# One exponential per head for the decay matrices, attention values two query blocks at a time, and modulated weights for the last down products

## The chip, the cores and the metric

The kernel runs on one core of a Trainium2 chip. The metric is the device time of one execution in microseconds. The engines are named as the profile names them: PE is TensorE (PEld its weight loads), DVE is VectorE, ACT is ScalarE, POOL is GpSimd, and SP issues the DMAs.

## The reference

One transformer block on 1024 tokens of width 1024. The parts that matter here:

```python
def _dilated_branch(q, k, v, rel_bias, window, dilation):
    ...
    s = jnp.einsum('bhrnqd,bhrnkd->bhrnqk', qb * dh ** -0.5, kw) + bias[None, :, None, None]
    s = jnp.where(valid, s, NEG_INF)
    ...
    o = jnp.einsum('bhrnqk,bhrnkd->bhrnqd', e, vw) / denom

def _chunk_gated_delta_rule(q, k, v, g, beta):
    ...
    diff = gcum[..., :, None] - gcum[..., None, :]
    decay = jnp.where(causal, jnp.exp(jnp.where(causal, diff, 0.0)), 0.0)
    k_beta = kc * bc[..., None]
    a_mat = jnp.where(strict, jnp.einsum('nbhcd,nbhed->nbhce', k_beta, kc) * decay, 0.0)
    ...
    qk = jnp.where(causal, jnp.einsum('nbhcd,nbhed->nbhce', qc, kc) * decay, 0.0)

def reference(...):
    ...
        y = jnp.concatenate([y_attn, y_delta], axis=-1) @ w_out[l]
        x = x + g1 * y
        h = _rmsnorm(x, norm_ffn_g[l]) * (1.0 + sc2) + sh2
        y = (jax.nn.silu(h @ w_gate[l]) * (h @ w_up[l])) @ w_down[l]
        x = x + g2 * y
    return _rmsnorm(x, final_norm_g)
```

`k` is l2-normalised per head before the delta rule, and the rows of `a_mat` and `qk` carry that norm's reciprocal root.

## The kernel before

The kernel is written against a tile framework that orders instructions ahead of time. Every instruction has a priority, its place in the program; a block under `urgent()` goes 6000 places ahead. A scheduler steps through a model of the chip and emits, on each engine, the ready instruction of the highest priority. The order so found is fixed: on the chip each engine runs its instructions in that order and waits wherever an operand is late. `tc.issue_after(ins)` ties an instruction behind another one on the same engine.

The work comes in stages. The first 100 us form the first projections. Then come two groups `g` of the gated delta rule, four heads each (`delta(0)`, `delta(1)`), then attention over four pairs of heads (`attend`), the output projection, the second norm, and the feed-forward network as seven products of a fast 2x2 scheme (`up_...` and `down`). The remaining projections of the input are a pool of filler, the generators behind `fill`. `ahead(us)` and `turn(name)` pull an amount of it into PE's stream where the table `FILL` has an entry, and attention draws what is left.

**Decay matrices.** For each group `delta_rows` (L697 on) broadcasts the cumulated gate G of each head over the partitions by a DMA into a tile `dt` of 128x8x128, and `affine_select` on POOL (L712) puts -1e30 below the diagonal. `delta_prep` (L750 on) takes the logarithm of the squared norms of k (`Ln`, L761, for group 0 at L1235), halves and negates it (L762), gets `rk` from it by `Exp` (L763) and subtracts G of the partition's own token (L764). The result `lr` is a bias per partition, one column per chunk and head, so 32 activations of 128x128 follow per group (L767): exp(G of the column + lr). Behind them on ACT stand two activations `eb` (L835). From `rk` come `nbp` (L771), which PE transposes (L777), `nbg` and `kds`. PE then forms the kk products (L796) and DVE multiplies them with the decay matrices (L802). POOL scales q with `eb` in place (L836). Conv and `Silu` of v stand in `delta_v` (L553, L557).

**Attention values.** A unit is a pair of heads `hp` and a block `qb` of 128 queries. `attend` runs score (L1325), softmax, transposes (L1349) with their copies into `et` tiles (L1352, L1354), and value products (L1366), the last three units behind the score. A unit's value products are 2(qb+1) matmuls of 128x64 by 128x128, the two heads e alternating and writing PSUM partitions 64e to 64e+63. Four `et` buffers exist, two to a unit.

**The last down products.** `down(i, ...)` runs one of seven products over 11 slices f; `down_parts` loads a slice of activations and weights and splits each into a high and a low part (L1603, L1604), and `down_mm` (L1809) makes three matmuls for each of four banks. In the last call, `down(6, ..., final=True)`, the last TAIL = 4 slices run bank by bank, each bank followed by its end: multiply with the gate g2 (L1858), add the residual (L1859), square with a sum (L1861), add the two half sums (L1867), root (L1868), reciprocal (L1869), scale (L1874, L1876) and store.

Of the kernel before, what the change touches and what calls it, by code (L numbers as in the profile page):

```python
# [18 lines left out]
P = 128  # L19
T = 1024  # L20
D = 1024
# [13 lines left out]
AHEADF = 3  # L35
XB, ETB, AT, AV = 5, 4, 1, 3
EPS = 1e-6
# [45 lines left out]
def build(tc, I, out):  # L83
# [466 lines left out]
    def conv(ci, xp, dst):  # L550
        nc.scalar.activation(dst, xp, AF.Copy, scale=cw[:, ci, 3:4])
        for s_ in range(1, 4):
            nc.vector.scalar_tensor_tensor(  # L553
                out=dst[:, s_:T], in0=xp[:, 0 : T - s_], scalar=cw[:, ci, 3 - s_ : 4 - s_], in1=dst[:, s_:T],
                op0=ALU.mult, op1=ALU.add,
            )
        nc.scalar.activation(dst, dst, AF.Silu)  # L557

# [138 lines left out]

    sel = {}

    def delta_rows(g):  # L700

        dts = []
        for hl_ in range(4):
# [10 lines left out]
                base=0, channel_multiplier=-1,  # L714
            )
            dts.append(dt_)
        return dts

    def delta_norms(g):
        n = {}  # L720
        for name in ("rk", "eq", "nbp", "nbg", "kds", "lr"):
            n[name] = pd.tile([P, 8, 4], F32, name=f"{name}{g}", tag=name, bufs=2)
        return n
# [26 lines left out]
    def delta_prep(g, st, norms, kt, lts):  # L750

        rk, eq, nbp, nbg, kds, lr = (norms[k] for k in ("rk", "eq", "nbp", "nbg", "kds", "lr"))
        gs = slice(32 * g, 32 * g + 32)
# [5 lines left out]

        if g == 1:  # L760
            nc.scalar.activation(lr, rk, AF.Ln, bias=eps1)  # L761
        nc.vector.tensor_scalar(out=lr, in0=lr, scalar1=-0.5, scalar2=None, op0=ALU.mult)  # L762
        nc.scalar.activation(rk, lr, AF.Exp)  # L763
        nc.vector.tensor_tensor(out=lr, in0=lr, in1=g3(Gc), op=ALU.subtract)  # L764
        for h in range(4):
            for n in range(8):
                nc.scalar.activation(lts[h][:, n], lts[h][:, n], AF.Exp, bias=lr[:, n, h : h + 1])  # L767
        nc.vector.tensor_scalar(
# [442 lines left out]
    def delta_early():  # L1211

        for j in range(4):
            kind, q = ("k", j) if j < 2 else ("q", j - 2)
            t = pr.tile([P, T], F32, name=f"cv{j}", tag="dt", bufs=2)
            conv((4 if kind == "k" else 0) + 2 + q, fetch(j, f"{kind}{2 + q}"), t)
            delta_turn(1, kind, q, t, norms=norms[1])
            nc.sync.dma_start(_.cv[j], t)
# [4 lines left out]
    def delta(g):  # L1223
        st = {}
        kt = []
        for j in range(4):
# [4 lines left out]
            if g == 0:  # L1231
                conv((4 if kind == "k" else 0) + hp, xps[j], t)
                kt.append(delta_turn(g, kind, q, t, norms=norms[0], keep=kind == "k"))
                if j == 1:
                    nc.scalar.activation(norms[0]["lr"], norms[0]["rk"], AF.Ln, bias=eps1)  # L1235
            else:
# [119 lines left out]

    def att_value(hp, qb, ets):
        va = loaded[hp][0]
        if qb % 4 == 0:
            ybanks[hp] = ybank(f"y{hp}_{qb}")  # L1360
        yps = ybanks[hp]
        yc = slice((qb % 4) * P, (qb % 4 + 1) * P)
        with turn(f"y{hp}_{qb}"):
            for kb in range(qb + 1):
                for e in range(2):
                    nc.tensor.matmul(  # L1366
                        yps[64 * e : 64 * e + 64, yc], va[:, kb, 64 * e : 64 * e + 64], ets[e][:, kb, :],
                        start=(kb == 0), stop=(kb == qb),
                    )
        if qb % 4 == 3:  # L1370
            cs = slice((qb - 3) * P, (qb + 1) * P)
# [421 lines left out]
    nc.sync.dma_start(gfr, I["gfin"].to_broadcast([P, D]))  # L1793

    def wdn_src(i, f):
        def at(j, s):
# [8 lines left out]
    def down_mm(bank, b, pr, f, first):  # L1805
        (ah, al_), (wh, wl) = pr
        ts_ = slice(b * P, (b + 1) * P)
        for n_, (a, w) in enumerate(((ah, wh), (ah, wl), (al_, wh))):
            nc.tensor.matmul(  # L1809
                bank[b], a[:, ts_], w, start=(first and f == 0 and n_ == 0), stop=(f == NF - 1 and n_ == 2),  # L1810
                skip_group_check=True,
            )

    ends = []

    def down(i, bank, first, end, final=False):
        pr = {}
        n = NF - TAIL if final else NF
        for f in range(NF):
            pr[f] = down_parts(i, f, pz if f >= n else None)  # L1820
            if f < n:
                for b in range(4):
                    down_mm(bank, b, pr[f], f, first)
            if f % 2 == 1 and ends:
                ends.pop(0)()
        assert not ends
        if final:
            with urgent():
                final = [end(b) for b in range(4)]
        for b in range(4):  # L1830
            if final:
                for f in range(n, NF):
                    down_mm(bank, b, pr[f], f, first)
                with urgent():
                    final[b]()
            else:
# [10 lines left out]
    rn = pz.tile([P, 8, 4], F32, name="rn", tag="rn")  # L1847
    dsl = [slice(s * HALF, (s + 1) * HALF) for s in range(2)]
    xr = {}

    def x_in(l, s, b):
        x = pz.tile([P, HALF], F32, name=f"xr{l}{s}{b}", tag="xr", bufs=4)
        nc.sync.dma_start(x, _.x2[l][b, :, dsl[s]])
        return x

    def half_end(l, s, b, src, t, x):

        nc.vector.tensor_tensor(out=t, in0=src, in1=g2r[:, dsl[s]], op=ALU.mult)  # L1858
        nc.vector.tensor_tensor(out=t, in0=t, in1=x, op=ALU.add)  # L1859
        sq = pz.tile([P, HALF], F32, name=f"sq3_{l}{s}{b}", tag="sq3", bufs=2)  # L1860
        nc.scalar.activation(sq, t, AF.Square, accum_out=rn[:, 4 * l + b, s : s + 1])  # L1861
        if s == l:
            nc.vector.tensor_tensor(out=t, in0=t, in1=gfr[:, dsl[s]], op=ALU.mult)

    def row_out(l, b):
        r = rn[:, 4 * l + b]
        nc.vector.tensor_tensor(out=r[:, 2:3], in0=r[:, 0:1], in1=r[:, 1:2], op=ALU.add)  # L1867
        nc.scalar.activation(r[:, 2:3], r[:, 2:3], AF.Sqrt, bias=eps1, scale=1.0 / D)  # L1868
        nc.vector.reciprocal(r[:, 3:4], r[:, 2:3])  # L1869
        tb = 4 * l + b  # L1870
        for s in (1 - l, l):
# [3 lines left out]
            else:  # L1875
                nc.vector.scalar_tensor_tensor(  # L1876
                    out=t, in0=t, scalar=r[:, 3:4], in1=gfr[:, dsl[s]], op0=ALU.mult, op1=ALU.mult
                )
            nc.sync.dma_start(out[tb * P : (tb + 1) * P, dsl[s]], t)

    def copy_end(dst, src):
        return lambda b: lambda: nc.scalar.copy(dst[b], src[b])

    def sum_end(l, s, src, other, row):


        def at(b):
            x = x_in(l, s, b)

            def go():  # L1890
                t = y[l, s][b]
                if other is not None:
                    add(t, src[b], other[b])
                half_end(l, s, b, src[b] if other is None else t, t, x)
                if row:
# [96 lines left out]
```

## Time and profile before

| | us |
|---|---|
| median of three runs | 1405.2 (1401.91 to 1408.69) |
| the profiled execution | 1407.41 |
| its span in the trace | 1405.6 |
| PE busy in the span | 1353.3 |
| DVE busy | 874.6 |
| ACT busy | 660.0 |
| POOL busy | 287.2 |

The profile is one execution. Its own time is 1.8 us above the span, which counts from the first to the last instruction of the program. A row of a stretch gives the busy time of each engine in it, the number of instructions in brackets, the clock that TensorE was granted (1.00 is full), the busy share of the DMA engines and their GB/s. A row of the timeline gives start, duration, engine, line, operation, output and inputs, shapes and count; what stands in square brackets is how long the engine sat idle before it, and what ended that.

### The profile page before, as it was taken

How to read it: one execution, taken by the hardware profiler on the slowest of the kernel's cores; microseconds unless marked ns; L12 is line 12 of the kernel's file. 1: busy time of each engine (PE TensorE's matmuls, PEld its weight loads, DVE VectorE, ACT ScalarE, POOL GpSimd, SP SyncE). 2: the span in 40 equal slices, each digit the busy share in tenths (PEclk: the TensorE clock that was granted, in tenths of full speed). 3: DMA queues.
4: the chain of work that ended last, by engine and by line, in shares of the span. 5: the costliest groups of instructions: out<-in, count | busy, mean ns of one | idle time of the engine just before them, and what ended most of it. 6: DMA issues, size and time to landing. Idle time of an engine off the chain costs nothing.

```text
span 1405.6 us, 24430 instructions
## 1 busy us (share of the span) xinstructions
PE 1353.3 (96%) x8984; PEld 1113.2 (79%) x8984; DVE 874.6 (62%) x1659; ACT 660.0 (47%) x1285; POOL 287.2 (20%) x261
## 2 busy tenths in 40 slices
PE   8998999998999999999999899999999999999997
PEld 4777787888889878777777678888888888888885
DVE  3688573656847242765248987666575776474487
ACT  4497424346233453765168533333333333444456
POOL 2344303324213433543262400000000000000000
PEclk9999999999999999999999999999999999999999
DMA  8666573475362555521675245444453665765566
GB/s 305 225 194 174 173 217 127 135 233 140 120 171 85 173 146 166 158 84 61 198 251 161 97 163 180 157 164 164 137 195 113 209 209 182 255 223 195 195 225 232
DMA packets 169872, 245.65 MB, mean 175 GB/s; under 512 B 32566, under 2 KB 73831, under 8 KB 169752
## 3 DMA queue, kind: packets, MB, share of 16 engines
q1 hardware_dynamic: 169752, 244.08, 54.2%
q8 instruction: 71, 1.16, 0.3%
q14 instruction: 49, 0.40, 0.1%
HBM read 181.27 MB, written 67.48 MB: 177 GB/s over the span
## 4 chain that ended last, share of the span: by engine, by line
PE 71%; DVE 13%; DMA 6%; ACT 4%; issue 3%; POOL 1%; SPq 0%; DVEq 0%; ACTq 0%; POOLq 0%
PE wua L1614 8%; PE wga L1614 8%; PE X L1809 6%; PE g_a L590 4%; PE wuc L1614 4%; PE Z L1809 4%; PE wgc L1614 4%; PE wo L590 3%; PE y L1366 2%; PE Y L1809 2%; PE tr L1349 2%; PE g_va L613 2%; DVE tm L896 2%; PE f L251 2%; PE wgb L1614 2%
## 5 line engine op out<-in xcount | busy, mean ns | idle before, releaser
L1604 DVE TENSOR_TENSOR wl_db<-wr_db,wh_db 128x512 fp32r<-128x512 f32 x77 | 53.2, 690 | 75.7 <-ACT wh_db L1603 75.6
L1603 ACT CAST wh_db<-wr_db 128x512 fp32r<-128x512 f32 x77 | 47.9, 622 | 97.7 <-PE X L1809 41.3
L1329 DVE CUSTOM_DVE_ANT_0 X<-S,ng 128x512 f32<-128x512 f32 (+3 forms) x64 | 36.6, 587 | 61.9 <-PE S L1326 46.4
L1809 PE MATMUL X<-wl_db,wh_da 128*128 128x512 f32 x176 | 68.6, 390 | 0.1
L1336 POOL TENSOR_SCALAR X<-X,sc 128x128 f32<-128x128 f32 (+7 forms) x64 | 50.0, 786 | 91.1 <-DVE sc L1335 77.7
L1809 PE MATMUL X<-wh_db,wl_da 128*128 128x512 f32 x176 | 68.5, 389 | 0.0
L1809 PE MATMUL X<-wh_db,wh_da 128*128 128x512 f32 x176 | 68.5, 389 | 0.0
L1334 ACT ACTIVATE X<-X,sc 128x128 f32<-128x128 f32 (+7 forms) x64 | 49.4, 773 | 33.9 <-DVE sc L1329 31.7
L1604 DVE TENSOR_TENSOR wl_da<-wr_da,wh_da 128x512 fp32r<-128x512 f32 x77 | 52.8, 686 | 1.6 <-ACT wh_da L1603 1.6
L590 PE MATMUL wo<-yh,wh_wo 128*128 128x512 f32 x128 | 51.7, 405 | 1.0 <-DVE xo L1417 1.0
L590 PE MATMUL g_a<-hh,wh_a 128*128 128x512 f32 x128 | 51.8, 404 | 0.0
L590 PE MATMUL wo<-yh,wl_wo 128*128 128x512 f32 x128 | 50.8, 397 | 0.0
L590 PE MATMUL wo<-yl,wh_wo 128*128 128x512 f32 x128 | 50.4, 394 | 0.1
L1603 ACT CAST wh_da<-wr_da 128x512 fp32r<-128x512 f32 x77 | 47.4, 616 | 6.4 <-PE wua L1614 5.9
L590 PE MATMUL g_a<-hl,wh_a 128*128 128x512 f32 x128 | 50.3, 393 | 0.0
L590 PE MATMUL g_a<-hh,wl_a 128*128 128x512 f32 x128 | 50.1, 392 | 0.0
L1603 ACT CAST wh_wg_s<-wg_s 128x512 fp32r<-128x512 f32 x33 | 20.5, 622 | 55.8 <-PE wuc L1614 23.8
L1349 PE MATMUL tr<-ident,X 128*128 128x128 f32 x288 | 42.9, 276 | 1.8 <-ACT et L1354 1.0
L1366 PE MATMUL y<-et,va 128*64 128x128 f32 x576 | 43.9, 280 | 0.0
L231 POOL TENSOR_TENSOR wl_wo<-wr_wo,wh_wo 128x512 fp32r<-128x512 f32 x24 | 32.5, 1357 | 51.7 <-ACT wh_wo L230 51.7
L1603 ACT CAST wh_wg<-wr_wg 128x512 fp32r<-128x512 f32 x31 | 19.3, 621 | 47.2 <-PE wua L1614 19.2
L1603 ACT CAST wh_wu_s<-wu_s 128x512 fp32r<-128x512 f32 x33 | 20.4, 622 | 44.5 <-PE wga L1614 17.5
(545 smaller groups left out, 4349.9 us busy)
## 6 DMA issues: line engine op xcount, KB each, us to landing
wm<-in_wada SPq DMA_DIRECT2D x44, 512.0 KB, 6.0
wr_da<-ao_d SPq DMA_DIRECT2D x77, 256.0 KB, 3.0
wr_wu<-in_wu SPq DMA_DIRECT2D x50, 256.0 KB, 2.8
wr_wg<-in_wg SPq DMA_DIRECT2D x48, 256.0 KB, 3.0
ao_d<-a SPq DMA_DIRECT2D x44, 256.0 KB, 2.6
wr_wd<-in_wdn SPq DMA_DIRECT2D x44, 256.0 KB, 3.0
wr_db<-wt_d SPq DMA_DIRECT2D x44, 256.0 KB, 2.7
ao_d<-as SPq DMA_DIRECT2D x33, 256.0 KB, 2.5
```

The source lines that it names most:

```text
L231: (eng or nc.gpsimd).tensor_tensor(out=lo[:, :n], in0=raw[:, :n], in1=hi[:, :n].bitcast(F32), op=ALU.subtract)
L251: nc.tensor.matmul(first[bank], a[:, w0], b[k][:, cs], start=(k == 0 and n_ == 0), stop=(k == KT - 1 and n_ == 2))
L590: last[0] = nc.tensor.matmul(ps, a[:, w0], b[k0 + k4][:, cs], start=(i == 0), stop=(i == n - 1))
L1329: nc.vector.tensor_tensor_reduce(out=X[:, c0:c1], in0=ps[:, 0 : c1 - c0], in1=ng[:, u + c0 : u + c1], scale=1.0, scalar=(3e38 if m is None ...
L1334: nc.scalar.activation(X[:, 0:nk], X[:, 0:nk], AF.Exp, scale=-1.0, bias=m, accum_out=sc[:, 2:3])
L1336: nc.gpsimd.tensor_scalar(out=X[:, 0:nk], in0=X[:, 0:nk], scalar1=sc[:, 3:4], scalar2=0.0, op0=ALU.mult, op1=ALU.add)
L1349: nc.tensor.transpose(ps[:, (kb - c0) * P : (kb - c0 + 1) * P], X[:, kb * P : kb * P + P], ident)
L1366: nc.tensor.matmul(yps[64 * e : 64 * e + 64, yc], va[:, kb, 64 * e : 64 * e + 64], ets[e][:, kb, :], start=(kb == 0), stop=(kb == qb),)
L1603: nc.scalar.copy(hi, src)
L1604: (eng or nc.vector).tensor_tensor(out=lo, in0=src, in1=hi.bitcast(F32), op=ALU.subtract)
L1614: nc.tensor.matmul(ps, a[:, w0], b, start=(first and k == 0 and n_ == 0), stop=(k == 3 and n_ == 2), skip_group_check=True,)
L1809: nc.tensor.matmul(bank[b], a[:, ts_], w, start=(first and f == 0 and n_ == 0), stop=(f == NF - 1 and n_ == 2), skip_group_check=True,)
```

## The change

Three edits that share no code.

*Decay matrices.* `delta_rows` subtracts G of the partition's token from each `dt` tile on DVE (128x1024, four per group). `delta_prep` takes `Sqrt` of the squared norms on ACT, tied behind the last `Silu` of the convolutions, and DVE's reciprocal; then one `Exp` of 128x1024 per head, in the order 3, 0, 1, 2 and tied to each other, and on DVE one multiplication of each tile with `rk` broadcast along the row. The `lr` tiles and the `Ln` go.

*Attention values.* `att_value` is called for odd `qb` alone and issues the products of `qb` and `qb - 1` together, under `urgent()`. The first two products are tied in order, and all others behind the second. The key blocks start with block 0 and then the last one (for qb = 7 with the last one). `ETB` goes from 4 to 6.

*Last down products.* The weights of the last four slices of product 6 are multiplied with g2 before they are split, and are loaded and split while product 5 runs (`held`). Their matmuls go to banks `W` of their own. While they run, the seven earlier slices in bank X are multiplied with g2 and added to the residual; the end of a bank is then one addition from PSUM, square, root, reciprocal, scale and store. The sums of squares are scaled by 1/1024 in the activation (scale 1/32 under the square), and the first half sum gets its epsilon ahead of time, so that `Sqrt` takes the other as its bias.

```diff
-XB, ETB, AT, AV = 5, 4, 1, 3
+XB, ETB, AT, AV = 5, 6, 1, 3
...
+            nc.vector.tensor_tensor(
+                out=dt_, in0=dt_, in1=bc(Gc[:, 32 * g : 32 * g + 32].rearrange("p (n h) -> p n h", n=8)[:, :, hl_], P),
+                op=ALU.subtract,
+            )
             dts.append(dt_)
...
-        if g == 1:
-            nc.scalar.activation(lr, rk, AF.Ln, bias=eps1)
-        nc.vector.tensor_scalar(out=lr, in0=lr, scalar1=-0.5, scalar2=None, op0=ALU.mult)
-        nc.scalar.activation(rk, lr, AF.Exp)
-        nc.vector.tensor_tensor(out=lr, in0=lr, in1=g3(Gc), op=ALU.subtract)
+        rkf = rk.rearrange("p n h -> p (n h)")
+        with tc.issue_after(silu[0].ins):
+            root = nc.scalar.activation(rkf, rkf, AF.Sqrt, bias=eps1)
+        nc.vector.reciprocal(rkf, rkf)
+        for h in (3, 0, 1, 2):
+            with tc.issue_after(root.ins):
+                root = nc.scalar.activation(lts[h], lts[h], AF.Exp)
         for h in range(4):
-            for n in range(8):
-                nc.scalar.activation(lts[h][:, n], lts[h][:, n], AF.Exp, bias=lr[:, n, h : h + 1])
+            nc.vector.tensor_tensor(out=lts[h], in0=lts[h], in1=bc(rk[:, :, h], P), op=ALU.mult)
...
-        with turn(f"y{hp}_{qb}"):
-            for kb in range(qb + 1):
-                for e in range(2):
-                    nc.tensor.matmul(
-                        yps[64 * e : 64 * e + 64, yc], va[:, kb, 64 * e : 64 * e + 64], ets[e][:, kb, :],
-                        start=(kb == 0), stop=(kb == qb),
+        seq = {q: (0, *range(q, 0, -1)) if q < 7 else (q, *range(q)) for q in (qb - 1, qb)}
+        parts = [(q, kb, e) for q in (qb, qb - 1) for kb in seq[q] for e in (1, 0)]
+        parts[1:2], parts[2:3] = parts[2:3], parts[1:2]
+        mm = None
+        with turn(f"y{hp}_{qb}"), urgent():
+            for i, (q, kb, e) in enumerate(parts):
+                with tc.issue_after(mm.ins) if i else ExitStack():
+                    ins = nc.tensor.matmul(
+                        yps[64 * e : 64 * e + 64, (q % 4) * P : (q % 4 + 1) * P],
+                        va[:, kb, 64 * e : 64 * e + 64], ets[q % 2][e][:, kb, :],
+                        start=(kb == seq[q][0]), stop=(kb == seq[q][-1]),
                     )
+                mm = ins if i < 2 else mm
...
-            if i >= AV:
+            if i >= AV and units[i - AV][1] % 2:
                 hp, qb = units[i - AV]
-                att_value(hp, qb, ets.pop(i - AV))
+                att_value(hp, qb, [ets.pop(i - AV - 1), ets.pop(i - AV)])
...
+        if p is not None:
+            with urgent():
+                nc.vector.tensor_tensor(out=b, in0=b, in1=g2r[:, dsl[0]], op=ALU.mult)
...
+            if i == 5 and f % 2 == 1 and len(held) < TAIL:
+                t = NF - TAIL + len(held)
+                held[t] = down_parts(6, t, pz)
...
+    def last_end(src, more):
+
+        def at(b):
+            x = x_in(1, 0, b)
+            t = y[1, 0][b]
+            nc.vector.tensor_tensor(out=t, in0=src[b], in1=g2r[:, dsl[0]], op=ALU.mult)
+            nc.vector.tensor_tensor(out=t, in0=t, in1=x, op=ALU.add)
+
+            def go():
+                nc.vector.tensor_tensor(out=t, in0=more[b], in1=t, op=ALU.add)
+                square(1, 0, b, t)
+                row_out(1, b)
+
+            return go
+
+        return at
...
-    down(6, X, False, sum_end(1, 0, X, None, True), final=True)
+    W = four("W")
+    down(6, X, False, last_end(X, W), tail=W)
```

More of the change, by code (lines that the diff above doesn't have):

```diff
@@ L698, in build @@
     sel = {}
+    silu = [None]
     def delta_rows(g):
@@ L750, in delta_prep @@
     def delta_prep(g, st, norms, kt, lts):
-        rk, eq, nbp, nbg, kds, lr = (norms[k] for k in ("rk", "eq", "nbp", "nbg", "kds", "lr"))
+        rk, eq, nbp, nbg, kds = (norms[k] for k in ("rk", "eq", "nbp", "nbg", "kds"))
         gs = slice(32 * g, 32 * g + 32)
@@ L1793, in build @@
     nc.sync.dma_start(gfr, I["gfin"].to_broadcast([P, D]))
+    dsl = [slice(s * HALF, (s + 1) * HALF) for s in range(2)]
     def wdn_src(i, f):
@@ L1809, in down_mm, with down @@
             nc.tensor.matmul(
-                bank[b], a[:, ts_], w, start=(first and f == 0 and n_ == 0), stop=(f == NF - 1 and n_ == 2),
-                skip_group_check=True,
+                bank[b], a[:, ts_], w, start=(first and n_ == 0), stop=(last and n_ == 2), skip_group_check=True,
             )
     ends = []
-    def down(i, bank, first, end, final=False):
+    held = {}
+    def down(i, bank, first, end, tail=None):
         pr = {}
[L1818 to L1823, printed above, removed]
+        n = NF - TAIL if tail else NF
+        for f in range(n):
+            pr[f] = down_parts(i, f)
+            for b in range(4):
+                down_mm(bank, b, pr[f], f, first and f == 0, f == n - 1)
+            if i == 5 and f % 2 == 1 and len(held) < TAIL:
+                t = NF - TAIL + len(held)
+                held[t] = down_parts(6, t, pz)
             if f % 2 == 1 and ends:
                 ends.pop(0)()
-        assert not ends
-        if final:
+        while ends:
+            ends.pop(0)()
+        if tail:
             with urgent():
-                final = [end(b) for b in range(4)]
+                last = [end(b) for b in range(4)]
         for b in range(4):
-            if final:
+            if tail:
                 for f in range(n, NF):
-                    down_mm(bank, b, pr[f], f, first)
+                    down_mm(tail, b, held[f], f, f == n, f == NF - 1)
                 with urgent():
-                    final[b]()
+                    last[b]()
             else:
@@ L1891, in go @@
                 t = y[l, s][b]
-                if other is not None:
-                    add(t, src[b], other[b])
-                half_end(l, s, b, src[b] if other is None else t, t, x)
+                add(t, src[b], other[b])
+                half_end(l, s, b, t, t, x)
                 if row:
```

30 lines of the change are left out of this document (14 added, 16 removed).

## The prediction

> **What bounds the kernel now.** I read the page first, then the busy time by stretches, then PE's waits, then the timeline around each of them.
>
> ```profile
> span 1405.6 us, 24430 instructions
> ...
> PE 1353.3 (96%) x8984; PEld 1113.2 (79%) x8984; DVE 874.6 (62%) x1659; ACT 660.0 (47%) x1285; POOL 287.2 (20%) x261
> ```
>
> PE is busy 96% of the span, so the whole of its idle time is 1405.6 - 1353.3 = 52.3 us. An edit off PE can win only a piece of that, or of the time that PE runs at a lower clock. An edit on PE wins what it takes out of the stream.
>
> ```profile
> 100.00:180.00 80.00, 72.65 (x524) 59.29 (x523) 54.67 (x77) 49.84 (x99) 32.87 (x22) 0.98 0.61 176
> ...
> 260.00:400.00 140.00, 130.49 (x1164) 119.11 (x1164) 92.74 (x201) 60.72 (x137) 47.17 (x38) 0.96 0.56 159
> ...
> 480.00:580.00 100.00, 98.59 (x625) 78.36 (x623) 40.36 (x123) 56.02 (x123) 41.34 (x39) 1.00 0.52 145
> ...
> 1386.00:1405.60 19.60, 10.46 (x45) 7.98 (x43) 11.36 (x26) 9.10 (x21) 0.00 (x0) 0.88 0.51 191
> ```
>
> The columns are stretch, length, then busy time of PE, PEld, DVE, ACT and POOL, clock, DMA. The decay matrices of group 0 lie in the first row (PE idle 7.35 us), those of group 1 in the second (9.51 us, clock 0.96), attention in the third (1.41 us idle), the end in the fourth (9.14 us idle). So attention can gain only inside PE's stream, and the other two edits only where PE waits.
>
> ```profile
> PE g_z L613 <- POOL wl_z L231: 3.1, 1, 3.1
> ...
> PE trv L872 <- ACT vd L557: 2.1, 2, 1.9
> PE ps_bp L777 <- DVE nbp L771: 2.0, 1, 2.0
> ```
>
> These three waits of PE lie around the decay matrices. The reader should follow the first one back.
>
> ```profile
> 322.81 8.58 ACT L767 ACTIVATE dt<-dt,lr 128x128 f32<-128x128 f32 x29
> 331.29 2.00 ACT L835 ACTIVATE eb<-eb 128x1024 f32<-128x1024 f32 x2
> ...
> 332.42 5.74 POOL L836 TENSOR_TENSOR qd<-qd,eb 128x1024 f32<-128x1024 f32 x2 [7.09 <-ACT eb L835]
> 338.10 2.25 POOL L231 TENSOR_TENSOR wl_z<-wr_z,wh_z 128x512 fp32r<-128x512 f32 x1
> ...
> 340.41 0.58 PE L613 MATMUL g_z<-wl_z,hh 128*128 128x256 f32 x1 [3.10 <-POOL wl_z L231]
> ```
>
> In group 1 ACT runs 29 small exponentials in one block; `eb` stands behind them, POOL's scaling of q waits for `eb` (7.09 us), the weight part `wl_z` stands behind that on POOL, and PE waits 3.10 us for `wl_z`. The wait has a second price, the clock (here PE's busy time and count, clock, DMA share, GB/s):
>
> ```profile
> 135.00:140.00 5.00, 4.85 (x39) 0.78 1.01 210
> 140.00:145.00 5.00, 5.00 (x60) 0.87 0.44 138
> ...
> 340.00:345.00 5.00, 4.59 (x21) 0.50 0.38 112
> 345.00:350.00 5.00, 5.00 (x41) 0.89 0.36 72
> ```
>
> After the wait PE runs at 0.50 and then 0.89: 5 x 0.50 + 5 x 0.11 = 3.05 us lost. After the wait for `nbp` in group 0 it is 0.78 and 0.87: 1.1 + 0.65 = 1.75 us. [...]
>
> **Part 1, decay matrices.** The exponentials:
>
> ```profile
> 136.88 8.57 ACT L767 ACTIVATE dt<-dt,lr 128x128 f32<-128x128 f32 x29
> ...
> 147.36 1.28 ACT L557 ACT_TABLE_LOAD   x1
> 148.66 1.06 ACT L557 ACTIVATE vd<-vd 128x1024 f32<-128x1024 f32 x1
> ...
> 149.77 1.09 PE L872 MATMUL trv<-ident,vd 128*128 128x128 f32 x8 [1.91 <-ACT vd L557]
> ```
>
> 29 of them take 8.57 us, 0.296 each, so 32 take 9.5 us. One of 128x1024 is bounded by `eb`: 2.00 us for two. Four take 4.0 us, and ACT is done 5.5 us sooner per group. `Ln` with its table goes and `Sqrt` with its table comes: nothing in this sum, since ACT is not what ends PE's waits there but what stands behind the exponentials.
>
> *Group 1.* `eb` does not need the multiplication with `rk`, so it moves up by the 5.5 us, and with it the scaling of q and `wl_z`: its end at 340.35 becomes 334.9, ahead of 340.41 - 3.10 = 337.31, where PE now begins to wait. The full prize is 3.10 + 3.05 = 6.15 us. What may hold it back: the scaling overwrites q, so it also needs the kk products done, and their banks are emptied by DVE (L802), which now has the new multiplications ahead of it. Bounds -6.15 and 0; I take two thirds, -4.1, because the row of POOL names `eb` as the releaser and not PE.
>
> *Group 0.* PE's 1.91 us before `trv` are behind `vd`'s `Silu`, behind a table load, behind `eb`. ACT would release them, but DVE is the neighbour:
>
> ```profile
> 121.70:149.10 27.40, 23.29 (x208) 19.58 (x206) 25.83 (x34) 24.22 (x54) 13.42 (x10) 0.94 0.70 186
> ...
> L553 DVE SCALAR_TENSOR_TENSOR vd<-xp_v,cw,vd x12: 1243/1286/2369, 125.4 to 351.3; 128x1023 f32<-128x1023 f32 x4, 128x1022 f32<-128x1022 f32 x4, 128x1021 f32<-128x1021 f32 x4
> ```
>
> DVE has 25.83 us of work in these 27.40. The change adds four subtractions and four multiplications of 128x1024. The trace has no such form at this place; the nearest row is the convolution's, two inputs of 128x1023, 1.286 us in the median and 2.369 at most. So 10.3 us are added at the median, 19.0 at the worst; the small steps L762 and L764 save 0.6. The products L802 then end 10.3 - 0.6 - 1.6 (idle) = 8.1 us late. What covers this is the filler, which PE draws from a fixed total, and the convolution of v, which can move between the subtractions and the multiplications while ACT works. I take 0; bounds -1.9 (the wait before `trv` gone) and, without cover, +8.1 and a dip of 1.75, +9.9. The subtractions also stand ahead of the convolution of v in DVE's order, and `vd`, its transposes and `vb` wait for that. In group 1 nothing is added for DVE's work, since DVE is idle for 10.39 us of the same stage there, and after group 0's products it is idle for 12.3 us until their rows come back by DMA:
>
> ```profile
> 300.00:338.00 38.00, 36.00 (x371) 32.24 (x369) 27.61 (x42) 32.87 (x68) 15.67 (x9) 1.00 0.77 214
> ```
>
> ```profile
> DVE nt L885 <- DMA nt<-lt_d: 12.3, 1, 12.3
> ```
>
> [...]
>
> Part 1: -4.1 us.
>
> **Part 2, values.** The number of products is the same. What changes is how often PE turns to them and away.
>
> ```profile
> 600.94 0.43 PE L1366 MATMUL y<-et,va 128*64 128x128 f32 x2
> 601.30 0.33 PE L1325 MATMUL S<-KS,QS 128*128 128x128 f32 x1
> ...
> 592.75 0.87 PE L1366 MATMUL y<-et,va 128*64 128x128 f32 x10
> 593.55 0.45 PE L1325 MATMUL S<-KS,QS 128*128 128x384 f32 x1
> ...
>   issue: 7.6, 36
> ```
>
> Two products hold PE's stream for 0.36 us (600.94 to 601.30), ten for 0.80 us. So a pair costs (0.80 - 0.36)/4 = 0.11 us, and the first pair 0.25 more. The last row is the weight loader's idle time before value products that nothing else explains: 36 times, 7.6 us, 0.21 each. I price a turn at 0.2 us. Under `urgent()` with all operands ready a pair of blocks runs in one piece, so 16 turns remain of at least 36: -20 x 0.2 = -4.0 us. Against it: the first two products are now of the same head e = 1, the halves no longer start in pairs, and one half-pair is left over at the end: one step of 0.11 us in each of 16 groups, +1.8 us. If it overlaps with the turn, it is free. Bounds -7.6 (all of that idle time goes) and +1.8 (the order still splits the groups). I take half of the left-over: -4.0 + 0.9 = -3.1 us. Two more `et` buffers cost space alone.
>
> **Part 3, the end.**
>
> ```profile
> 1396.18 0.39 PE L1809 MATMUL X<-wh_db,wl_da 128*128 128x512 f32 x1
> ...
> 1397.49 0.68 DVE L1858 TENSOR_TENSOR y<-X,g2r 128x512 f32<-128x512 f32 x1
> ...
> 1399.29 0.63 ACT L1861 ACTIVATE sq<-y 128x512 f32<-128x512 f32 x1 [0.38 <-DVE rn L1869]
> ...
> 1400.53 0.28 ACT L1868 ACTIVATE rn<-rn,eps 128x1 f32<-128x1 f32 x1
> ...
> 1401.04 0.75 DVE L1876 SCALAR_TENSOR_TENSOR y<-y,rn,gfr 128x512 f32<-128x512 f32 x1
> ...
> 1336.30:1366.20 29.90, 29.90 (x133) 24.77 (x132) 23.57 (x39) 15.03 (x31) 0.00 (x0) 1.00 0.70 228
> ```
>
> PE's last product ends at 1396.57, the last scaling starts at 1401.04: 4.47 us, of which 0.92 pass before DVE takes the bank at all. Afterwards there remain the addition (0.68, bounded by L1858, also from PSUM), the square from 1399.29 to the root at 1400.53 (1.24, less the addition of half sums that goes, some 0.3), and the root to the scaling, 0.51: 0.68 + 0.94 + 0.51 = 2.1 us. Gain 2.3 us. Price: four more multiplications and eight splits on DVE during product 5, 12 x 0.61 = 7.3 us (0.68 less 0.07 of overlap), where DVE has 29.90 - 23.57 = 6.3 us free. They are covered but for 1.0 us, and the ends of product 4 can wait that long before bank X is needed; without that, PE waits 1.0 us. Bounds -2.3 and +1.0; I take -2.3, because the ends have 19 us of product 6 to catch up in before the last chain begins (its seven earlier slices, at 29.90 us for eleven).
>
> **Sum.** -4.1 - 3.1 - 2.3 = -9.5 us against the profiled execution: span 1396.1, own time 1397.9. It ran at 1407.41, 2.2 us above the median shown, so against the median of 1405.2 I write 1395.7.
>
> **Rivals.**
> 1. *The wait only moves* (0.17). PE still finds something late in group 1, since DVE got the time that ACT gave up. Parts 2 and 3 alone: -5.4, 1399.8 us. For it: DVE's 25.83 of 27.40. Against it: group 1's chain runs over ACT and POOL.
> 2. *DVE becomes the bound of group 0* (0.12). The eight new operations meet POOL, 1.286 to 2.369 each, the decay products end 8.1 to 16.8 us late, and PE stands at the kk products, whose banks are not emptied, because the fixed order has no filler there; group 1 gains nothing. At the middle, 12.4 + 1.75 - 5.4 = +8.8: 1414 us. It decides from about 5.4 us of waiting on. For it: POOL is busy 13.42 us of that stretch. Against it: the 12.3 us in which DVE idles behind these products, so lateness there has room.
> 3. *The groups stay split* (0.08). The change does not do what it says in attention: part 2 costs 1.8 instead, -4.6 in all, 1400.6 us. For it: the order is found in a model of the chip and not on it. Against it: a block under `urgent()` outranks whatever else is ready.
> 4. *All of it* (0.12). Both waits of PE and both dips go: 6.15 + 1.9 + 1.75 = 9.8, with 3.1 and 2.3: 1390.0 us. For it: all of them lie behind the exponentials or the norms on ACT. Against it: `nbp` still waits for a root on ACT.
>
> **Chances.** The forecast has 0.51, with its own range 1391 to 1399. About 0.5%, 7 us, is what a measurement of this kernel can tell from no change. Below 1398.2 lie four fifths of the forecast (0.41), rival 4 (0.12) and some 0.07 of rivals 1 and 3: 0.60 faster. Slower is rival 2, 0.12. The rest, 0.28, is the same. The range 1384 to 1407 holds all but rival 2 and some 0.06 at its two ends.
>
> **What would show it.** Right: 8 activations of 128x1024 at the decay lines of about 1.0 us; no wait of PE for `wl_z` and no clock of 0.50 after it; 16 runs of value products; 2 us from PE's last product to the last scaling. Wrong: PE waiting for DVE at L796 or L777 for several microseconds, or a clock dip at a new place; DVE operations of over 2 us at the new lines; over 30 runs of value products; the last scaling over 4 us behind PE.

## The result, and the profile after

The changed kernel takes 1413.27 us in the median of nine runs (1408.38 to 1415.92), beside 1405.5 before: ratio 1.0047, 95% interval [1.0029, 1.0064], by the ratio some 6.6 us slower. A second set of twelve runs gave 1.0021 [1.0004, 1.0038], 3.0 us. The forecast was 1395.7 and faster; the range ended at 1407.

The page of the changed kernel (first line and busy times):

```profile
span 1406.6 us, 24338 instructions
...
PE 1347.0 (96%) x8984; PEld 1109.2 (79%) x8984; DVE 905.0 (64%) x1681; ACT 648.4 (46%) x1227; POOL 291.2 (21%) x261
```

PE and ACT are busy for less than before (1347.0 for 1353.3, 648.4 for 660.0), DVE for 30.4 us more, and the span is no shorter. The profiled execution took 1408.38 us, the least of the nine; the others ran up to 7.5 us longer. So the trace shows where the time goes, and the interval how much it is.

The same four stages, the last one shifted by the 1 us that the span has grown (stretch, length, busy time of PE, PEld, DVE, ACT and POOL, clock, DMA share, GB/s):

```profile
100.00:180.00 80.00, 69.13 (x501) 55.70 (x502) 63.30 (x74) 41.15 (x65) 38.64 (x22) 0.96 0.58 163
260.00:400.00 140.00, 129.21 (x1087) 118.93 (x1089) 103.77 (x213) 53.84 (x104) 45.97 (x39) 0.98 0.54 154
480.00:580.00 100.00, 96.84 (x615) 78.41 (x613) 33.96 (x116) 50.91 (x116) 39.30 (x39) 1.00 0.51 140
1387.00:1406.60 19.60, 12.97 (x57) 10.35 (x56) 11.16 (x21) 7.05 (x17) 0.00 (x0) 0.88 0.45 170
```

In the first, PE is idle for 10.87 us (7.35 before) and DVE has 8.6 us more; in the second PE is idle for 10.79 (9.51) and DVE has 11.0 us more. In the third, attention, it is idle for 3.16 (1.41), and its waits for DVE's `sc` are 2.7 us in all for 0.7. At the end it is idle for 6.63 (9.14). PE's own waits:

```profile
PE kk_q L802 <- DVE nbpT L785: 5.9, 2, 3.5
...
PE st L1001 <- DVE S L1034: 3.7, 1, 3.7
...
PE ps_bp L783 <- DVE nbp L777: 2.1, 1, 2.1
...
PE Z L1823 <- DVE wl_db L1613: 1.5, 3, 0.6
```

The wait for `wl_z` is gone. Of these waits for DVE two are new, 5.9 us for `nbpT` and 1.5 for `wl_db`, and one has grown: the longest for the state `S` was 1.4 before and is 3.7. The one for `nbp` stood before, with 2.0. The first, on DVE's timeline in group 0, with the copy's row of before ahead of it:

```profile
136.22 0.27 DVE L779 COPY nbpT<-ps_bp 32x128 f32<-32x128 f32 x1
```

```profile
121.03 1.23 DVE L717 TENSOR_TENSOR dt<-dt,Gc 128x1024 f32<-128x1024 f32 x1 [1.18 <-POOL dt L713]
...
128.03 5.94 DVE L717 TENSOR_TENSOR dt<-dt,Gc 128x1024 f32<-128x1024 f32 x3
...
137.84 6.33 DVE L773 TENSOR_TENSOR dt<-dt,rk 128x1024 f32<-128x1024 f32 x3
144.10 0.30 DVE L218 STREAM_TRANSPOSE t<-tri 128x128 f32<-128x128 f32 x1
144.33 2.05 DVE L773 TENSOR_TENSOR dt<-dt,rk 128x1024 f32<-128x1024 f32 x1
146.30 0.15 DVE L222 TENSOR_TENSOR mod<-t,bada 128x4 f32<-128x4 f32 x1
146.38 0.17 DVE L774 TENSOR_SCALAR eq<-eq 128x32 f32<-128x32 f32 x1
146.46 0.18 DVE L780 TENSOR_TENSOR nbg<-nbp,eG 128x32 f32<-128x32 f32 x1
146.56 0.27 DVE L785 COPY nbpT<-ps_bp 32x128 f32<-32x128 f32 x1
```

Read the second block from the bottom. The copy that empties the bank of the transposed `nbp` is done at 146.83, some 10 us later than before, and PE, which needs the bank for the kk products, starts at 146.89 after 3.54 us. The copy takes 0.27 us; what is ahead of it are the four multiplications, 8.4 us in all, and ahead of these three subtractions of 5.9 us. One of the eight is 1.23 us long, where POOL is idle; three in a row take 2.0 or 2.1 each in the mean. These are means of unlike operations: over both groups single ones last from 1.21 to 2.93 us.

The second wait, first on DVE, then on PE, and last PE's wait at the same place before:

```profile
258.03 2.27 DVE L717 TENSOR_TENSOR dt<-dt,Gc 128x1024 f32<-128x1024 f32 x1 [6.18 <-POOL dt L713]
260.32 0.95 DVE L1034 COPY S<-st 64x64 f32<-64x64 f32 x4
```

```profile
260.93 0.46 PE L1001 MATMUL st<-S,kd 128*128 128x128 f32 x2 [3.72 <-DVE S L1034]
```

```profile
260.41 0.48 PE L995 MATMUL st<-S,kd 128*128 128x128 f32 x2 [1.40 <-DVE S L1030]
```

This is group 0's scan, and the subtraction is group 1's. It stands ahead of the state copies in DVE's order, DVE waits 6.18 us in front of it for POOL's masking (which waits 3.41 us for its DMA), and PE waits for the state. Behind both waits the clock falls (PE's busy time first, clock third from the end):

```profile
145.00:150.00 5.00, 3.11 (x24) 3.11 (x25) 4.63 (x10) 0.00 (x0) 1.26 (x2) 0.59 0.25 68
150.00:155.00 5.00, 4.20 (x40) 3.72 (x37) 5.00 (x6) 1.06 (x1) 1.40 (x1) 0.72 0.28 82
...
260.00:265.00 5.00, 4.07 (x21) 3.85 (x21) 3.06 (x12) 0.53 (x2) 1.81 (x2) 0.70 0.50 166
265.00:270.00 5.00, 5.00 (x28) 4.81 (x27) 2.82 (x10) 0.74 (x2) 0.61 (x1) 0.62 0.08 26
```

Where the decay part's work is over stands the first attention score product, here before and after:

```profile
458.81 0.30 PE L1325 MATMUL S<-KS,QS 128*128 128x128 f32 x1
```

```profile
464.36 0.31 PE L1329 MATMUL S<-KS,QS 128*128 128x128 f32 x1
```

It comes 5.6 us late. That is one trace beside one; the experiments show how far this mark moves between traces.

In group 1 PE stands 2.39 us before the kk products for the same copy (the second of the two in 5.9), where it stood 3.10 for `wl_z`. And `wl_z` did not come in time by the path that was forecast. `eb` was to move up by 5.5 us and to bring the scaling of q and `wl_z` with it:

```profile
328.83 1.29 POOL L231 TENSOR_TENSOR wl_z<-wr_z,wh_z 128x512 fp32r<-128x512 f32 x1 [0.98 <-ACT wh_z L230]
...
342.65 2.01 ACT L841 ACTIVATE eb<-eb 128x1024 f32<-128x1024 f32 x2
...
343.78 4.76 POOL L842 TENSOR_TENSOR qd<-qd,eb 128x1024 f32<-128x1024 f32 x2 [7.64 <-ACT eb L841]
```

`eb` starts 11.4 us later than before (342.65 for 331.29). The scheduler has put `wl_z` ahead of the scaling of q in POOL's order, where it stood behind it.

The tail, on DVE, behind PE's last product (starts 1399.58, ends 1399.97):

```profile
1400.01 0.69 DVE L1910 TENSOR_TENSOR y<-W,y 128x512 f32<-128x512 f32 x1
1401.82 0.16 DVE L1889 RECIPROCAL rn<-rn 128x1 f32<-128x1 f32 x1 [1.12 <-ACT rn L1888]
1402.01 0.75 DVE L1896 SCALAR_TENSOR_TENSOR y<-y,rn,gfr 128x512 f32<-128x512 f32 x1
```

2.04 us to the last scaling, where it was 4.47.

### The profile page after: what moved, and what is told of

It reads as the page before. It is cut to its first block, busy times and chain, and to the rows that moved or that the text cites. A ratio compares the mean times of both kernels' runs of the same rounds, so it can differ in the third digit from the quotient of the medians.

```text
span 1406.6 us, 24338 instructions
## 1 busy us (share of the span) xinstructions
PE 1347.0 (96%) x8984; PEld 1109.2 (79%) x8984; DVE 905.0 (64%) x1681; ACT 648.4 (46%) x1227; POOL 291.2 (21%) x261
## 4 chain that ended last, share of the span: by engine, by line
PE 69%; DVE 16%; DMA 4%; issue 4%; ACT 3%; POOL 2%; SPq 0%; DVEq 0%; ACTq 0%; POOLq 0%
PE wga L1623 8%; PE wua L1623 8%; PE X L1823 6%; PE wo L590 4%; PE wuc L1623 4%; PE wgc L1623 4%; PE g_a L590 4%; PE Z L1823 3%; PE Y L1823 2%; DVE tt L906 2%; PE y L1374 2%; PE f L251 2%; PE wgb L1623 2%; PE wub L1623 2%; PE tr L1353 2%
## 5 line engine op out<-in xcount | busy, mean ns | idle before, releaser
L1823 PE MATMUL X<-wl_db,wh_da 128*128 128x512 f32 x160 | 62.4, 390 | 0.3 <-DVE wl_db L1613 0.3
L1823 PE MATMUL X<-wh_db,wh_da 128*128 128x512 f32 x160 | 62.3, 389 | 0.0
L1823 PE MATMUL X<-wh_db,wl_da 128*128 128x512 f32 x160 | 62.3, 389 | 0.0
L1353 PEld LDWEIGHTS tr<-ident,X 128*128 128x128 f32 x288 | 32.7, 140 | 15.2 <-POOL X L1340 5.1
```

What stands on the lines that cost most here:

```text
L1353: nc.tensor.transpose(ps[:, (kb - c0) * P : (kb - c0 + 1) * P], X[:, kb * P : kb * P + P], ident)
L1823: nc.tensor.matmul(bank[b], a[:, ts_], w, start=(first and n_ == 0), stop=(last and n_ == 2), skip_group_check=True,)
```

## The experiments

All ratios are against the kernel before on the same chip; 1% is 14 us. Line numbers differ a little from kernel to kernel.

**One part at a time.** The diff's hunks for the decay matrices alone (e1), for the values alone (e2), for the end alone (e3).

> The decay part alone; values and down products as before. Theory: the loss of the whole change sits here. VectorE gets eight operations of 128x1024 more in group 0, which take 2.0 to 2.1 us each beside GpSimd, and the emptying of the bank of the transposed nbp stands behind the last four. So the profile should show TensorE's wait at the kk products (3.5 us in group 0, 2.4 in group 1), the start of the first attention scores about 5.6 us later than before, and a time 5 to 11 us above before (ratio 1.004 to 1.008), the upper end if the clock dips more often than in the one profile. Rival 'attention pays': the decay part is worth what was forecast, -4 us (ratio 0.997), and the time is lost in the regrouped value products. Rival 'sum of small losses': +1 to +3 us here, the rest in the other two.

> The value products of two query blocks in one group, nothing else. Theory: 16 runs of value products for 47, -3 to -5 us (ratio 0.9965 to 0.998), no new wait. Rival 'attention pays': above before by 3 us or more (ratio over 1.002), with the granted clock lower in attention. Forecast of the blind prediction: -3.1 us.

> The held down products alone. Theory: the tail behind TensorE's last product is 2.4 us shorter (9.0 to 6.6), but TensorE waits for VectorE's weight splits in product 5 at three or four places, in all 2 to 3 us, so that the sum is -0.5 to +1 us (ratio 0.9997 to 1.0007). Rival 'the split work is covered': no wait for the splits in product 5, -2.3 us (ratio 0.9984).

| part | ratio | interval | us |
|---|---|---|---|
| decay (e1) | 1.0065 | [1.0041, 1.0090] | +9.1 |
| values (e2) | 0.9961 | [0.9937, 0.9985] | -5.5 |
| down (e3) | 0.9999 | [0.9978, 1.0019] | -0.1 |

The loss sits in the decay part, and the parts add up to +3.5, between the two measurements of the whole (+6.6 and +3.0); each part is known to about 3 us. In e1 the same two waits stand (6.0 us at the kk products, 3.4 for S), and scores start at 465.1.

For the values, the weight loader's idle time before them is the witness:

```profile
  ACT et L1354: 3.4, 10
  issue: 0.8, 3
```

"issue" was 7.6 us in 36 pieces. What is left waits for probabilities, 3.4 us in 10 pieces that were not there before, so half of what the grouping took away came back. The value products now make 16 runs in the trace (47 before). From the first score to the first product `x2t` behind the output projection, the six traces with the values part (change, e9, e2, e8, e11, e12) take 241.6 to 244.1 us and the ten without it 245.8 to 249.0: some 5 us, which agrees with the -5.5 of the times.

For the end, product 5 of e3 (second row) and the stretch ahead of it (first row):

```profile
1301.90:1331.90 30.00, 30.00 (x134) 24.86 (x133) 14.96 (x24) 13.51 (x25) 0.00 (x0) 1.00 0.60 193
1331.90:1363.50 31.60, 30.96 (x134) 24.33 (x133) 29.56 (x53) 19.14 (x38) 0.00 (x0) 1.00 0.82 276
```

Product 5 takes 1.7 us longer than the 29.90 of before, with DVE at 29.56 of 31.60. In the whole change it takes 32.7, with PE's three waits for `wl_db`. The seven slices of product 6 behind it take 19.7 us in e3, 0.7 more than in e10 below, where PE has no such wait. Together that is about the tail's 2.4 us. Product 4 beside it has half of DVE free (busy for 14.96 of 30.00 us).

**The held parts in product 4.**

```diff
-            if i == 5 and f % 2 == 1 and len(held) < TAIL:
+            if i == 4 and f % 2 == 1 and len(held) < TAIL:
```

> The held down products alone, prepared in product 4 of the down phase. Theory: the tail's 2.4 us remain and the waits for the splits in product 5 go: -2 to -3 us (ratio 0.998 to 0.9985), against -0.1 in the place of the change. Rival 'the tail is not worth its 2.4 us': within 1 us of before.

0.9977 [0.9955, 1.0000], -3.2 us. Products 4 and 5:

```profile
1304.40:1334.40 30.00, 30.00 (x134) 24.82 (x134) 22.05 (x35) 17.46 (x32) 0.00 (x0) 1.00 0.80 261
1334.40:1364.40 30.00, 30.00 (x134) 24.86 (x133) 23.88 (x43) 15.24 (x31) 0.00 (x0) 1.00 0.70 228
```

PE never stops in either, and the time agrees with a tail that is worth its 2.4 us, though the interval ends at 1.0000. So the cover is there in product 4, and the change had put the work into the product that had too little.

**The order on DVE or its sum?** e4 moves the four multiplications behind the copy and its DMA:

```diff
-        for h in range(4):
-            nc.vector.tensor_tensor(out=lts[h], in0=lts[h], in1=bc(rk[:, :, h], P), op=ALU.mult)
...
         nc.sync.dma_start(_.bp[g], nbpT)
+        for h in range(4):
+            nc.vector.tensor_tensor(out=lts[h], in0=lts[h], in1=bc(rk[:, :, h], P), op=ALU.mult)
```

> The decay part alone, with the four multiplications by rk written behind the emptying of the nbp bank and its DMA. Theory that the order of VectorE's queue makes the wait: the bank is emptied some 6 us sooner, TensorE's wait of 3.5 us at the kk products goes or moves to the rk multiplications as smaller ones, and the time falls by 2 to 4 us against the decay part alone. Rival 'VectorE's sum is what is late': the subtraction at the kk banks comes no sooner, the wait only changes its name, and the time is within 1 us of the decay part alone.

1.0068 [1.0043, 1.0094]: no better than e1's 1.0065. The wait for the copy is down to 1.0 us in one place, but the clock in these 15 us is 0.67, 0.50 and 0.81:

```profile
135.00:140.00 5.00, 3.46 (x19) 2.96 (x19) 5.00 (x10) 4.22 (x6) 3.33 (x2) 0.67 0.87 206
140.00:145.00 5.00, 5.00 (x43) 3.46 (x41) 5.00 (x4) 1.32 (x3) 3.69 (x2) 0.50 0.39 86
145.00:150.00 5.00, 5.00 (x26) 3.86 (x23) 5.00 (x7) 2.40 (x4) 1.45 (x2) 0.81 0.80 258
```

DVE is busy for 15.00 of 15.00 us. The wait of 3.5 us is gone and the first product behind these stages (`lv`) comes at the same time (223.4 us for e1's 223.6). My expectation that the order makes the wait is refuted as far as the time goes; the rival, that DVE's sum is what is late, stands. A kernel with less of that sum, e6, leaves the four multiplications out (a constant takes the place of `rk` in the exponent):

> The decay part alone without its four multiplications by rk in each group; the exponential has a constant bias of -4 in their place, so the output is not the reference's. Theory 'VectorE's sum is late': VectorE loses 8 us of work in group 0, TensorE's wait at the kk products is under 1 us in both groups, the first attention scores start 3 us or more earlier than in the decay part alone, and the time is 3 to 7 us below it. Rival 'order on ScalarE and the table loads': the time stays within 2 us of the decay part alone.

1.0015 [0.9991, 1.0040], 7 us less than e1. The waits at the kk products are 1.8 us for 6.0. The scores start at 465.4 in its trace, no earlier than in e1, where 3 us earlier was expected; the marks below show where this trace gains and loses.

**The subtraction ahead of the scan.** e5 holds group 1's subtractions back until the last convolution but one of its k and q on DVE:

```diff
+            with tc.issue_after(steps[-2].ins) if g else ExitStack():
                 nc.vector.tensor_tensor(
```

where `steps` is a list of the convolutions' last DVE instructions.

> The decay part alone, with group 1's four subtractions held back on VectorE until the last convolution of its early k and q, so that none of them stands ahead of the state copies of group 0's scan. Theory: TensorE's wait of 3.4 us for the state S (257.9 to 261.2 in the decay part alone) falls back to the 1.4 us of before, the dip behind it to its old length, and the first attention scores start 3 to 4 us earlier; 3 to 4 us below the decay part alone (1415.0). Rival 'late scan': the wait is there because group 0 comes late as a whole, it stays at over 3 us with another releaser, and the time is within 1 us of the decay part alone.

1.0045 [1.0027, 1.0063], +6.3 us for e1's +9.1; the intervals overlap. The waits:

```profile
PE kk_q L805 <- DVE nbpT L788: 6.0, 2, 3.6
...
PE st L1004 <- DVE S L1039: 3.5, 3, 2.1
```

The wait for S falls from 3.4 in one to 2.1, where 1.4 was expected, and products of `g_va` start at 269.5 for 274.4. But the scores start at 464.7, not 3 to 4 us earlier, since PE runs the 10 us from 330 on at 0.50 in this trace, where e1's has the full clock. Its worth, about 3 us, is the difference of two ratios here. Then the two of them together (e13), and no new work on DVE at all (e14: neither subtractions nor multiplications, again a constant in the exponent):

> The decay part alone with group 1's subtractions held back and without the multiplications by rk (constant bias of -4 in the exponential; the output is not the reference's). Theory that these two make up the loss: the single cuts gave -3 and -7 us against before's +9, so together -1 to +2 us against before (ratio 0.999 to 1.0015). Rival 'a third cost is left in the decay part' (its table loads, the four subtractions of group 0): +4 us or more (ratio 1.003 or more).

> The decay part alone with neither subtractions nor multiplications: one exponential of 128x1024 per head with a constant bias of -4, no new work on VectorE at all (the output is not the reference's). It shows what ScalarE's shorter block is worth by itself. The blind forecast's gain stands if it is -4 us or more against before (ratio 0.997 or less). Theory: there was little to gain even so, since what ends the waits is VectorE's chain; 0 to -3 us (ratio 0.998 to 1.000). Rival: above before, so that part of the loss is ScalarE's own order and table loads (ratio over 1.002).

e13: 0.9992 [0.9964, 1.0020]. With both mechanisms out the decay part costs nothing; no third cost is left that these runs could tell. The four kernels agree with each other: the multiplications cost 7.0 us with the subtraction ahead of the scan (e1 less e6) and 7.4 without (e5 less e13), its place 2.8 (e1 less e5) and 3.2 (e6 less e13). e14: 0.9980 [0.9956, 1.0004]. ACT's shorter block alone, unpaid by DVE, is worth 2.8 us, and the interval reaches from -6.2 to +0.6. Of these three waits in its trace the last one is new, and it is for DVE:

```profile
PE g_z L615 <- ACT zt L636: 3.4, 2, 1.8
PE st L997 <- DVE S L1032: 2.9, 3, 1.5
PE kk_q L798 <- DVE dt L804: 2.7, 1, 2.7
```

Three marks show where the loss arises. At each of them PE has done the same number of products in every kernel, so the start of the mark (us) is how late PE is:

| decay part | `lv`, behind group 0's kk products | first `g_va`, in group 0's scan | first score |
|---|---|---|---|
| as before (before, e2, e3, e8, e10) | 218.1 to 221.0 | 263.7 to 268.1 | 453.5 to 461.6 |
| changed (change, e9, e1) | 223.0 to 225.1 | 274.1 to 274.4 | 464.4 to 466.7 |
| subtraction late (e5) | 223.2 | 269.5 | 464.7 |
| no multiplications (e6) | 220.1 | 269.4 | 465.4 |
| both (e13) | 219.6 | 265.3 | 454.2 |

Up to `lv` the multiplications make PE some 4 us late, and from there to `g_va` the subtraction another 4; e5 and e6 each keep one of the two and e13 neither. From `g_va` to the first score all these kernels take between 188 and 197 us, those with the change 190 to 192: as far as this spread lets one see, group 1 shows neither a loss nor the gain that was forecast. The 8 us between kernels that share the decay part of before say how little one trace's score tells, and e5 and e6 lose behind `g_va` what they had gained.

**Half of the new work.** e7 is the kernel before with `lr` added by DVE and one exponential per head: four new operations a group for the change's eight.

```diff
         for h in range(4):
-            for n in range(8):
-                nc.scalar.activation(lts[h][:, n], lts[h][:, n], AF.Exp, bias=lr[:, n, h : h + 1])
+            nc.vector.tensor_tensor(out=lts[h], in0=lts[h], in1=bc(lr[:, :, h], P), op=ALU.add)
+            nc.scalar.activation(lts[h], lts[h], AF.Exp)
```

> Before with one exponential per head, but the logarithm of the norm is kept: VectorE adds lr to each matrix (four new operations per group for the change's eight), and 4 exponentials of 128x1024 take the place of 32. Theory: the price goes with VectorE's added work, so this costs half of the decay part or less: 0 to +4 us against before (ratio 1.000 to 1.003). Rival 'any shortening of ScalarE's block pays': -3 us or more (ratio under 0.998). Rival 'the exponentials themselves': the same +9 us as the decay part.

0.9987 [0.9968, 1.0006], no difference. None of the new operations, -2.8; four, -1.8 here, -1.1 in e13 and, with one of them ahead of the scan's copies, +2.1 in e6; all eight, +6.3 in e5 and, with one ahead of the scan's copies, +9.1 in e1 (each to about 3 us): the first four are paid by what ACT gives up, the next four are not.

**The whole once more, and versions that keep what pays.** e9 is the changed kernel again; e8 has the values and the held parts in product 4; e11 is e8 with e7's edit, e12 with e7's edit in group 1 alone.

> The changed kernel once more, beside the three below. Theory: 5 to 10 us above before (ratio 1.003 to 1.007), the sum of the parts measured alone: decay +9, values -5, down 0 would give +4; what is above that comes from dips of the granted clock, which this second profile should show in stages that the first ran at 1.00. Rival 'the parts act on one another': above +10 us.

> The values part and the held down products, but with the held parts prepared in product 4 of the down phase, for product 5. Theory: the values part gives -4.5 us; the tail gives 2.4 us, and product 4 has VectorE time free that product 5 has not, so that TensorE's three waits for the splits (0.6 us each) go: 1398 to 1400 us (ratio 0.995 to 0.996). Rival 'no cover in product 4 either': waits of the same size at another place, 1401 to 1402 us.

> Values, held parts in product 4, and one exponential per head with lr added on VectorE, in both groups. Theory: the adds cost on VectorE about what ScalarE's shorter block gives, -1.8 to +2 us against the same without it (1398.3), so 1396 to 1400 us. Rival 'ScalarE's block is what counts once VectorE has only four operations more': 1394 us or less.

> The same with the one exponential per head in group 1 only, where VectorE idles for 10.4 us of the stage and ScalarE's block stands ahead of the weight part wl_z. Theory: TensorE's wait of 3.1 us for wl_z and its dip go and nothing is paid in group 0: 2 to 5 us below 1398.3, so 1393 to 1396 us. Rival 'the wait only moves' (the blind prediction's first): within 1.5 us of 1398.3, with a wait of TensorE for VectorE at the kk products of group 1.

| kernel | median us | ratio | interval |
|---|---|---|---|
| change again (e9) | 1411.50 | 1.0021 | [1.0004, 1.0038] |
| values + held in product 4 (e8) | 1398.26 | 0.9931 | [0.9904, 0.9959] |
| the same + lr added (e11) | 1399.00 | 0.9943 | [0.9924, 0.9961] |
| the same + lr added in group 1 (e12) | 1397.62 | 0.9943 | [0.9911, 0.9975] |

For e9 I expected 5 to 10 us above before; it was 3.0, near the sum of the parts. Its trace has the same waits as the first (5.9 and 3.5 us) at a span of 1411.1 and a mean clock of 0.985 for 0.991. Taken over all stretches of 5 us up to 1400 with a clock under 0.97, length times the missing clock is 18.9 us in it and 10.3 in the first: the 4.5 us between the two executions are within what the clock takes. e8 beats both kernels: 0.7% below the one before, about 1% below the changed one; e11 and e12 can't be told from it. e12 answers what group 1 could give:

```profile
PE kk_q L800 <- DVE nbpT L783: 3.4, 1, 3.4
```

The wait of 3.1 us for `wl_z`, which e8 still has, is gone, and this one stands in its place. My expectation of 2 to 5 us there was wrong; the rival was right.

## Why the prediction was wrong, step by step

**Part 1, group 0: this step failed.** "I take 0", with bounds from -1.9 to +9.9. The working had the cost (10.3 to 19.0 us for eight operations; 15.6 by the rows above) and the lateness (8.1 us or more). What failed is the cover. "The filler, which PE draws from a fixed total" is too short where PE stood: PE runs some 5.6 us of it between 137.71 and 143.36 and then has nothing for 3.54 us, since the bank that the kk products need is emptied by a DVE copy behind all four multiplications. With that copy ahead of them (e4) the wait goes and the time stays: what is late is DVE's sum, and without the multiplications (e6) 7 us come back. The count of free DVE time, 27.40 less 25.83, had said that eight operations don't fit.

Rival 2 named the mechanism ("DVE becomes the bound of group 0", POOL beside it, PE standing at the kk products); it was given 0.12. That its time, 1414, is near the 1413.3 and 1411.5 measured is in part luck: by the ratios the change costs 6.6 and 3.0 us where rival 2 had 8.8, and it put 14 us on the decay part, which costs 9.1, of which some 3 are the scan's, which it did not name. The row of DVE spoke for it. Its 1.286 to 2.369 us for an operation were an estimate from the convolution's row. The trace of the change agrees: 1.23 us where POOL is idle, and 2.0 and 2.1 in the mean of the two threes, during which POOL is busy for 4.85 of 5.94 and for 5.01 of 6.33 us. What makes an operation longer there, no run separates. Against it spoke DVE's 12.3 us of idle time later. That later room is no cover for PE, which waits earlier.

**A step that was left out.** The subtraction was counted as four operations per group and not as a place in DVE's queue. In group 1 the first of them stands in the middle of group 0's scan, and the scan's state copies stand behind it. The cost was worked out for the stage where the results are used and not for the one where the instructions stand: 3.7 us of wait, about 3 us of time by e5 and by e13.

**Part 1, group 1: -4.1 did not come.** `wl_z` came in time, but by luck: `eb` did not move up, POOL's order changed. The dip of clock at 340 to 350 was gone in the first trace (in e9's there is one of 0.53 and 0.78 at 335 to 345). "In group 1 nothing is added for DVE's work" failed: DVE's idle time of that stage does not lie ahead of the copy that PE needs. The first rival's "wait only moves" is what happened: the copy of `nbpT` behind a DVE with new work. e12 shows it with half the work, e14 that even with none the whole part is worth -2.8 (-6.2 to +0.6), less than the 4.1 that group 1 alone was to give, though the interval doesn't exclude it.

**Part 2: right.** -3.1 forecast, -5.5 [-8.9, -2.1] measured; 16 runs and 0.8 us of idle "issue" time. The grouping took nearly all of that idle time, 6.8 us and not 4.0, and new waits for probabilities, which the working did not have, brought 3.4 back. That the forecast lies inside the interval owes something to these two errors of opposite sign. What is left of the 5 us between the traces, behind 3.4 of idle time, no row here explains; the left-over half-pair can't be told.

**Part 3: mechanism right, the price mis-sized.** 2.1 us from the last product to the last scaling was forecast, 2.04 measured. The price was worked out (7.3 us of work for 6.3 free) and then set to nothing, since the ends could catch up. Product 5 grew from 29.9 to 31.6 us alone and 32.7 in the whole, more than the 1.0 bounded. PE's new waits there are for `wl_db`, the splits of its next slice: DVE is busy for 29.56 of 31.60 us in e3, and the new work, issued behind every second slice, stands among them. Product 4 has the room: DVE is busy there for 14.96 of 30.00 us in e3, and with this work for 22.05 in e10, where PE never stops.

## What to carry to other kernels

When work moves from one engine to another, find what the bound engine waits for on the receiving one, and count all that must be done there before it, in the stage where the instruction is issued and not where its result is used. Pulling one small instruction forward is no cure if the sum behind it is late as well: in e4 it won nothing (1.0068 for e1's 1.0065). Sums of free time prove that something doesn't fit; they never prove that it does. A part that pays should be measured alone before it is bundled: here one of three parts paid, a second pays one product earlier, and the third hid them.

## What was not expected of the hardware

A very small DVE operation lasted longer, while POOL worked, than a large one lasts alone (1.23). `eq` on 128x32 took 0.17 us at 146.38 (above) and 1.89 in group 1, under POOL's scaling of kt:

```profile
332.39 1.89 DVE L774 TENSOR_SCALAR eq<-eq 128x32 f32<-128x32 f32 x1
```

```profile
332.31 3.83 POOL L827 TENSOR_TENSOR kt<-kt,kds 128x1024 f32<-128x1024 f32 x2
```

3.83 for two is 1.9 each, and the second starts at 334.20: the small operation, which ends at 334.28, ends with the first of them. So the 0.6 us that the prediction credited for small steps was no constant either.

And removing a wait of PE did not return its time where the next stretch then ran at half clock: e4 is without e1's wait of 3.5 us at the kk products of group 0, and its clock falls to 0.67, 0.50 and 0.81 in the 15 us from 135 on; e1 has the wait, and then 0.61 and 0.71 in the 10 us from 145 on. No run here separates what starts these dips.
